# Residual update and norm by token tile, with the transposes queued behind set shares of context products

## The chip, the cores and the metric

The kernel is one program on one core of a Trainium2 chip. The metric is device time in microseconds. Before the change the median of three runs is 1722.03 us (1718.5 to 1724.54). The profile shown here was taken from one more execution, which took 1722.1 us.

## The reference, cut to what matters

256 tokens of 1024 features pass through two blocks, each with two layers. In the first block a layer is

```
u = rms_norm(h, g_mix_pre[i]);  y = mixer_i(u)          # i=0 stick-breaking, i=1 dilated
h = h + rms_norm(y, g_mix_post[i])
u = rms_norm(h, g_ffn_pre[i]);  f = relu(u @ w_ff_in)**2 @ w_ff_out
h = h + rms_norm(f, g_ffn_post[i])
h = h + (p[i] @ w_ple[i]) * sigmoid(rms_norm(h, g_ple[i]) @ w_ple_gate[i])
```

In the second block a layer works on the tokens and on 256 context tokens. Six rows of modulation per stream (shift, scale, gate, twice) come from a product of a condition vector:

```
u = rms_norm(h) * (1 + scale) + shift;  h = h + gate * mixer(u, context)   # i=0 MLA + pooling, i=1 grouped-query
u = rms_norm(h) * (1 + scale) + shift;  h = h + gate * conv_ffn(u)
```

The context goes through the same layer of its own at i=0 and gives keys and values at both. The result is the tokens after a last rms_norm with a gain. All is float32.

## The kernel before

**Products.** The 256 tokens are two tiles of 128, called tt = 0 and 1. Every float32 product is done as three products of rounded parts (`mm3`, L195 to L197: high by high, low by high, high by low). A weight block comes by a DMA that SyncE issues (`ws`, four buffers), is rounded on ScalarE (`wh`, L183), and VectorE subtracts to get the rest (`wl`, L184). Activations are split alike (`put_split`, L200 and L201). A normalised activation is transposed on TensorE into a PSUM bank of 512 columns (`flip_group`, L231), four transposes of 128 columns for a group, two groups for a token tile, and each group is then split into `uh` and `ul`. There are two banks `mm` and two banks `fx`.

**Stages.** On the main path the order is stick mixer, FFN, gate from p ("ple"), dilated mixer, FFN, ple, MLA, gated FFN ("ffn2"), grouped-query attention ("gqa"), gated FFN. Between two of them stands a stage end: the residual update from the two accumulators `acc` (`post_norm`, `gated_add`, or the end of `ple`), then `main_norm`, which makes the next `u` and transposes it. Both tiles are updated first, then both are normed, and each group's transposes are issued as soon as that half of `u` is made.

**Context work as filler.** The context's products and the modulation products (`fx` banks) don't hang on the main path. They are generators in the queues `ctx` and `mod`. `fill(n)` adds n microseconds' worth of credit and issues steps while the credit is above zero; each step takes its worth away. `FILL[...]` holds the amounts: after `main_norm` comes `fill(FILL["mix0"])` and so on for mix1 (8.5 each), post0 9.6, post1 12.0, ple0 and ple1 10.0, f2 15.0, pre2 8.5. A scheduler then orders each engine's instructions by readiness and priority, so transposes and filler products end up interleaved. `tc.issue_after(x)` adds an edge that holds what is issued under it behind instruction x. At the end of the last gqa stage and after it no context work is left.

**Second layer's context.** `ctx_norm` reads the context, `xc`, back from DRAM, where the end of the context's FFN at i=0 has written it (L1256, L1194), norms it tile by tile and transposes into the `fx` banks. `ffn2(0)` issues filler after each chunk until that norm is issued.

**Rows.** Gains, shifts and gates are loaded by `row`, broadcast over the partitions, 512 KB each, into one pool of two buffers; so the third row's DMA waits for the readers of the first. SyncE issues DMAs in the order written by the scheduler, and one that waits holds those behind it.

**The lines.** `post_norm` (L519) is a rstd, a mul and a scalar_tensor_tensor; `gated_add` is L527 and L528; the norm's Square is L223, its tensor_scalar L215, the power on GpSimd L217, the gain L245, and the last step L252 or L254.

Of the kernel before, what the change touches and what calls it, by code (L numbers as in the profile page):

```python
# [101 lines left out]
def two_block_kernel(ctx: ExitStack, tc: tile.TileContext, a: dict, out: bass.AP, dbg=None):  # L102
# [90 lines left out]

    def mm3(o, lh, ll, rh, rl, start, stop):
        pe.matmul(o, lh, rh, start=start, stop=False)  # L195
        pe.matmul(o, lh, rl, start=False, stop=False)  # L196
        pe.matmul(o, ll, rh, start=False, stop=stop)  # L197
# [44 lines left out]
    def norm_one(src, g, shift, f, tt, bank):  # L242
# [4 lines left out]
        c0 = 0  # L247
        for grp in f.groups:
            w = grp[0].shape[1] * 128
            s = slice(c0, c0 + w)  # L250
# [36 lines left out]
    def tok_blocks(y, us, blocks, first, last):  # L287

        for tt in range(2):
            ts = slice(tt * 128, (tt + 1) * 128)  # L290
            for k, ((uh, ul), (bh, bl)) in enumerate(zip(us, blocks)):
                for nh in range(2):
                    s = slice(nh * 512, nh * 512 + 512)
                    mm3(y[tt][:, s], uh[:, ts], ul[:, ts], bh[:, 0, s], bl[:, 0, s],
                        first and k == 0, last and k == len(us) - 1)
# [410 lines left out]
    def ple(i, u, pw):  # L706
        y = lin_tok(u, KC, a["w_ple_gate"][i])
        for tt in range(2):
            t = tmp()
            act.activation(out=t, in_=y[tt], func=AF.Sigmoid)  # L710
            vec.tensor_mul(out=t, in0=t, in1=pw[:, tt, :])
            vec.tensor_add(out=h[:, tt, :], in0=h[:, tt, :], in1=t)

# [694 lines left out]
    u = main_norm(g_first)  # L1408

    for i in range(2):  # L1410
        y = stick(u) if i == 0 else dilated(u)
        g = row(a["g_mix_post"][i])
        for tt in range(2):
            post_norm(y[tt], g, tt)
        save(f"h{i}a", h)
        u = main_norm(row(a["g_ffn_pre"][i]))
        fill(FILL[f"mix{i}"])
        with tc.tile_pool(name="pl", bufs=1) as p:
            pf = []
            y = ffn1(i, u, lambda: pf.append(ple_in(i, p)))  # L1420
            pw = ple_mm(i, p, pf[0])
            g = row(a["g_ffn_post"][i])
            for tt in range(2):
                post_norm(y[tt], g, tt)
            save(f"h{i}b", h)
            u = main_norm(row(a["g_ple"][i]))
            fill(FILL[f"post{i}"])
            until_dense(FILL[f"dp{i}"])
            ple(i, u, pw)
        save(f"h{i}c", h)  # L1430
        if i == 0:
            u = main_norm(row(a["g_mix_pre"][1]))
            fill(FILL["ple0"])
    u = main_norm(mod_row(0, 0, 1), mod_row(0, 0, 0))
    fill(FILL["ple1"])
# [14 lines left out]
    for i in range(2):  # L1450
        if i == 1:
            u = main_norm(mod_row(1, 0, 1), mod_row(1, 0, 0))
            fill(FILL["pre2"])
            y = gqa(u)
        g = mod_row(i, 0, 2)
        for tt in range(2):
            gated_add(y[tt], g, tt)
        save(f"xl{i}a", h)
        u = main_norm(mod_row(i, 0, 4), mod_row(i, 0, 3))
        fill(FILL["f2"])  # L1460
        y = ffn2(i, u)
        g = mod_row(i, 0, 5)
        for tt in range(2):
            gated_add(y[tt], g, tt)
        save(f"xl{i}b", h)
    g = row(a["g_final_2"])
    for tt in range(2):
        r = rstd(h[:, tt, :], D)
        t = tmp()
        vec.scalar_tensor_tensor(out=t, in0=h[:, tt, :], scalar=r, in1=g, op0=ALU.mult, op1=ALU.mult)  # L1470
        nc.sync.dma_start(out=out[0, tt * 128:(tt + 1) * 128, :], in_=t)
# [33 lines left out]
```

## Time and profile before

| | |
|---|---|
| median of three runs | 1722.03 us (1718.5 to 1724.54) |
| profiled execution: time, span | 1722.1 us, 1720.3 us |
| TensorE busy, matmuls | 1635.5 us, 95% |
| VectorE busy | 1211.1 us, 70% |
| ScalarE busy | 926.6 us, 54% |
| GpSimd busy | 44.6 us, 3% |
| DMA moved, mean | 337.65 MB, 196 GB/s |
| mean granted clock of TensorE | 0.988 of full |

A page gives the busy time of each engine, the span in 40 slices, and the chain of work that ended last. PE is TensorE's matmuls and PEld its weight loads, DVE VectorE, ACT ScalarE, POOL GpSimd, SP SyncE. In a timeline row the bracket is the idle time of that engine ahead of the row, with what ended it. Names are those of the program, without buffer numbers.

### The profile page before, as it was taken

The page shows a single profiled execution, that of the slowest core. Times are in us where ns is not written, and L with a number is a line of the kernel's source. Part 1 is how long each engine was busy: PE and PEld are TensorE (multiplying, and loading weights), DVE is VectorE, ACT ScalarE, POOL GpSimd, SP SyncE. Part 2 cuts the span into 40 slices and gives each one's busy share as a digit, 9 for nine tenths or more (in the row PEclk, how much of TensorE's full clock was granted, in tenths as well). Part 3 has the DMA queues.
Part 4 walks back from the last instruction along what each step waited for, and adds up shares of the span by engine and source line. Part 5 has one row for each costly group of instructions (what it writes and reads, how often), then busy time and mean ns, then how long its engine had stood idle before and what let it go on. Part 6 is the DMA issues. An engine that isn't in the chain of part 4 may idle for free.

```text
span 1720.3 us, 28310 instructions
## 1 busy us (share of the span) xinstructions
PE 1635.5 (95%) x10259; PEld 1428.7 (83%) x10260; DVE 1211.1 (70%) x2251; ACT 926.6 (54%) x1854; POOL 44.6 (3%) x69
## 2 busy tenths in 40 slices
PE   7998999999999999989989999999999999989997
PEld 6767888887788879877978898888989987779997
DVE  4437777678788886767767866867686687676665
ACT  5536555545655556544446555764555555545554
POOL 0000000000000000000000000000000000000000
PEclk9999999999999999999999999999999999989999
DMA  7777666665766665777876555345776664246662
GB/s 240 259 257 232 203 217 214 207 217 165 241 186 205 185 188 160 242 236 245 280 231 208 176 172 174 115 136 180 233 239 205 185 187 148 72 153 187 186 187 98
DMA packets 301039, 337.65 MB, mean 196 GB/s; under 512 B 18384, under 2 KB 246164, under 8 KB 300900
## 3 DMA queue, kind: packets, MB, share of 16 engines
q1 hardware_dynamic: 300900, 335.86, 62.4%
q8 instruction: 80, 1.31, 0.3%
q14 instruction: 59, 0.48, 0.1%
HBM read 332.56 MB, written 3.23 MB: 195 GB/s over the span
## 4 chain that ended last, share of the span: by engine, by line
PE 55%; DVE 14%; DMA 13%; issue 4%; ACT 3%; SPq 1%; POOL 1%; ACTq 0%; POOLq 0%; DVEq 0%
PE mm L195 6%; PE mm L196 6%; PE mm L197 6%; PE acc L197 6%; PE acc L196 6%; PE acc L195 6%; DMA ws<-in_w_mod 6%; DVE wl L184 5%; PE fx L195 4%; PE fx L196 4%; PE fx L197 4%; DMA ws<-in_w_ff_in 2%; DVE ga L497 2%; DMA ws<-in_w_in_dil 2%; ACT wh L183 1%
## 5 line engine op out<-in xcount | busy, mean ns | idle before, releaser
L184 DVE TENSOR_TENSOR wl<-ws,wh 128x512 fp32r<-128x512 f32 (+1 forms) x1004 | 638.1, 668 | 273.3 <-ACT wh L183 261.5
L183 ACT CAST wh<-ws 128x512 fp32r<-128x512 f32 (+1 forms) x1004 | 568.6, 604 | 477.8 <-PE mm L196 132.7
L197 PE MATMUL mm<-uh,wl 128*128 128x256 f32 x1344 | 382.9, 285 | 8.4 <-DVE wl L184 8.1
L195 PE MATMUL mm<-uh,wh 128*128 128x256 f32 x1344 | 382.3, 284 | 0.3
L196 PE MATMUL mm<-ul,wh 128*128 128x256 f32 x1344 | 381.5, 284 | 0.0
L197 PEld LDWEIGHTS mm<-uh,wl 128*128 128x128 f32 x1344 | 258.6, 192 | 11.5 <-DVE wl L184 11.0
L195 PEld LDWEIGHTS mm<-uh,wh 128*128 128x128 f32 x1344 | 258.7, 193 | 5.0 <-DVE ul L201 0.9
L196 PEld LDWEIGHTS mm<-ul,wh 128*128 128x128 f32 x1344 | 258.7, 193 | 2.6
L195 PE MATMUL acc<-wh,hh 128*128 128x512 f32 x432 | 172.1, 399 | 0.0
L196 PE MATMUL acc<-wl,hh 128*128 128x512 f32 x432 | 171.3, 397 | 0.0
L197 PE MATMUL acc<-wh,hl 128*128 128x512 f32 x432 | 170.2, 394 | 0.0
L497 DVE SCALAR_TENSOR_TENSOR ga<-ws,cst,ga 128x1024 f32<-128x1024 f32 x84 | 106.3, 1281 | 57.7 <-DMA ws<-in_w_mod 57.5
L195 PE MATMUL fx<-uch,wh 128*128 128x256 f32 x352 | 102.2, 290 | 0.0
L197 PE MATMUL fx<-uch,wl 128*128 128x256 f32 x352 | 100.9, 287 | 0.0
L196 PE MATMUL fx<-ucl,wh 128*128 128x256 f32 x352 | 100.5, 286 | 0.0
L197 PEld LDWEIGHTS acc<-wh,hl 128*128 128x128 f32 x432 | 81.9, 190 | 18.9 <-issue 1.2
L195 PEld LDWEIGHTS acc<-wh,hh 128*128 128x128 f32 x432 | 82.2, 190 | 17.6 <-issue 1.6
L196 PEld LDWEIGHTS acc<-wl,hh 128*128 128x128 f32 x432 | 82.3, 191 | 14.5
L195 PE MATMUL mm<-wh,uh 128*128 128x384 f32 (+1 forms) x256 | 85.3, 333 | 1.9 <-ACT wh L183 1.1
L196 PE MATMUL mm<-wl,uh 128*128 128x384 f32 (+1 forms) x256 | 83.0, 324 | 0.3 <-DVE wl L184 0.3
L197 PE MATMUL mm<-wh,ul 128*128 128x384 f32 (+1 forms) x256 | 82.0, 322 | 0.0
L217 POOL TENSOR_TENSOR s<-s,neghalf 128x1 f32<-128x1 f32 (+2 forms) x52 | 39.9, 767 | 1452.9 <-DVE s L215 1413.1
(405 smaller groups left out, 2705.8 us busy)
## 6 DMA issues: line engine op xcount, KB each, us to landing
ws<-in_ffn_w_up SPq DMA_DIRECT2D x528, 128.0 KB
ws<-in_w_mod SPq DMA_DIRECT2D x96, 512.0 KB
ws<-in_ffn_w_down SPq DMA_DIRECT2D x66, 512.0 KB
ws<-in_w_ff_in SPq DMA_DIRECT2D x64, 512.0 KB
ws<-in_w_ff_out SPq DMA_DIRECT2D x64, 512.0 KB
ws<-in_w_in_dil SPq DMA_DIRECT2D x96, 192.0 KB
ws<-in_w_in_sb SPq DMA_DIRECT2D x24, 512.0 KB
row<-mod SPq DMA_DIRECT2D x19, 512.0 KB
```

Source lines behind the costliest of these rows:

```text
L183: act.copy(out=h[:, s], in_=st[:, s])
L184: vec.tensor_sub(out=l[:, s], in0=st[:, s], in1=f32(h[:, s]))
L195: pe.matmul(o, lh, rh, start=start, stop=False)
L196: pe.matmul(o, lh, rl, start=False, stop=False)
L197: pe.matmul(o, ll, rh, start=False, stop=stop)
L217: gp.tensor_tensor(out=r, in0=v, in1=neghalf.to_broadcast([128, w]), op=ALU.pow)
L497: vec.scalar_tensor_tensor(out=o, in0=st, scalar=c, in1=o, op0=ALU.mult, op1=ALU.add)
```

## The change

1. `norm_vec` makes both halves of `u` for one tile without transposing. `main_norm` now takes the residual update as `pre` and does update and norm for tile 0, then for tile 1.
2. `fill_dense(n)` issues context steps worth n microseconds and gives back the last matmul. In `main_norm` tile 0's eight transposes are held behind the last matmul of a share FILL − 2.2, tile 1's eight behind that of a second share of 2.2; then comes `fill(2.2 + what was left)`. `fill_dense` sets the credit to what it has spent, so it is negative when it returns.
3. `gated_norm` loads the gate of the second block's residual updates into a pool of its own, opened after the stage before has closed its pools.
4. `tok_blocks` sorts a last block by output half. gqa's last output blocks are (4), (5, 6, 7) where they were (4), (5), (6, 7).
5. The first step: x's tile 0, the identity, the gain and then x's tile 1 are loaded in this order, and tile 1 is transposed into the `fx` banks.
6. The last step: gated update, sum of squares, scaling and output go by halves of 512 columns.

```diff
+    def norm_vec(src, g, shift):
         u = tmp()
         if shift is not None:
             vec.tensor_mul(out=u, in0=src, in1=g)
         r = rstd(src, D)
+        for s in (slice(0, 512), slice(512, 1024)):
...
-            flip_group(u[:, s], grp, tt, bank)
-            c0 += w
+        return u
@@ tok_blocks
-            for k, ((uh, ul), (bh, bl)) in enumerate(zip(us, blocks)):
-                for nh in range(2):
...
+            steps = [(k, nh) for k in range(len(us)) for nh in range(2)]
+            if last:
+                steps.sort(key=lambda x: x[1])
+            for k, nh in steps:
...
+    def fill_dense(n):
+
+        clean("mod")
+        last_mm[0] = None
+        while n > 0 and queues["ctx"] and dense[0] > 0.1:
+            before = credit["ctx"]
+            fill_step("ctx")
+            n -= before - credit["ctx"]
+        credit["ctx"] = min(credit["ctx"], 0.0)
+        return last_mm[0], n
@@ first loads
+    nc.sync.dma_start(out=ident, in_=ca[:, C_ID:C_ID + 128])
+    g_first = row(a["g_mix_pre"][0])
     nc.sync.dma_start(out=h[:, 1, :], in_=a["x"][0, 128:256, :])
-    g_first = row(a["g_mix_pre"][0])
-    nc.sync.dma_start(out=ident, in_=ca[:, C_ID:C_ID + 128])
@@ gqa
-            for ks in ((4,), (5,), (6, 7)):
+            for ks in ((4,), (5, 6, 7)):
@@
-    def main_norm(g, shift=None):
+    def main_norm(g, shift=None, pre=None, n=(0.0, 0.0, 0.0), banks=(mm1, mm1)):
+
         u = Feat(m4, KC, "u")
+        toks, left = [], 0.0
         for tt in range(2):
-            norm_one(h[:, tt, :], g, shift, u, tt, mm1)
+            if pre:
+                pre(tt)
+            toks.append(norm_vec(h[:, tt, :], g, shift))
+        for tt in range(2):
+            ins, more = fill_dense(n[tt] + left) if n[tt] else (None, 0.0)
+            left = max(more, 0.0)
+            with tc.issue_after(getattr(ins, "ins", ins)) if ins is not None else nullcontext():
+                to_T(toks[tt], u, tt, banks[tt])
+        fill(left + n[2])
         return u
...
+    def filler(name):
+        return (FILL[name] - 2.2, 2.2, 2.2)
+
+    def gated_norm(y, i, m, j, k, name):
+
+        with tc.tile_pool(name="rw", bufs=1) as p:
+            gate = p.tile([128, D], F32, name="gate")
+            nc.sync.dma_start(out=gate, in_=mod[i][0, m * D:(m + 1) * D].partition_broadcast(128))
+            return main_norm(mod_row(j, 0, k + 1), mod_row(j, 0, k), pre=behind(y, gate, gated_add), n=filler(name))
 
     for i in range(2):
         y = stick(u) if i == 0 else dilated(u)
-        g = row(a["g_mix_post"][i])
-        for tt in range(2):
-            post_norm(y[tt], g, tt)
+        u = main_norm(row(a["g_ffn_pre"][i]), pre=behind(y, row(a["g_mix_post"][i]), post_norm), n=filler(f"mix{i}"))
         save(f"h{i}a", h)
-        u = main_norm(row(a["g_ffn_pre"][i]))
-        fill(FILL[f"mix{i}"])
...
@@ last step
+        for nh in range(2):
+            s = slice(nh * 512, nh * 512 + 512)
+            vec.tensor_mul(out=t[:, s], in0=y[tt][:, s], in1=gate[:, s])
+            vec.tensor_add(out=h[:, tt, s], in0=h[:, tt, s], in1=t[:, s])
+            act.activation(out=j[:, s], in_=h[:, tt, s], func=AF.Square, accum_out=ss[:, nh:nh + 1])
...
+        for nh in range(2):
+            s = slice(nh * 512, nh * 512 + 512)
+            vec.scalar_tensor_tensor(out=t[:, s], in0=h[:, tt, s], scalar=r, in1=g[:, s], op0=ALU.mult, op1=ALU.mult)
+            nc.sync.dma_start(out=out[0, tt * 128:(tt + 1) * 128, s], in_=t[:, s])
```

Three places show what the edit does to the order of the instructions.

TensorE before, at the end of the first mixer: `fx` are context products, the rows with `ident` are transposes of `t`, the normed tile 0.

```order
L197 MATMUL fx<-wh,ucl 128x512
L231 MATMUL mm<-ident,t_1948 128x128 x4
L195 MATMUL fx<-wh,uch 128x512
L231 MATMUL mm<-ident,t_1948 128x128 x4
L196 MATMUL fx<-wl,uch 128x512
L197 MATMUL fx<-wh,ucl 128x512
L195 MATMUL fx<-wh,uch 128x512
L196 MATMUL fx<-wl,uch 128x512
L197 MATMUL fx<-wh,ucl 128x512
L195 MATMUL fx<-wh,uch 128x512
L231 MATMUL mm<-ident,t_1972 128x128 x4
```

Each group of four transposes has products of the filler behind it. Tile 1's two groups follow in the same way, and six products of filler stand between the second of tile 0 and the first of tile 1.

TensorE after, at the same place, the end of the second share; `t_1958` is the normed tile 1, and `mm<-uh` are the FFN's own products.

```order
L197 MATMUL fx<-wh,uch 128x512
L198 MATMUL fx<-wl,uch 128x512
L199 MATMUL fx<-wh,ucl 128x512
L233 MATMUL mm<-ident,t_1958 128x128 x8
L197 MATMUL mm<-uh,wh 128x256
L198 MATMUL mm<-ul,wh 128x256
L199 MATMUL mm<-uh,wl 128x256
```

All eight transposes of a tile stand together, 36 filler products are ahead of tile 0's and 12 between the tiles, and behind tile 1's the FFN's own products follow with no filler between.

SyncE before, from the last weights of the first gated FFN on: `gr` is a gain of the gqa stage, `row` a shift or a scale.

```order
L177 DMA ws<-in_ffn_w_down 128x1024 x3
L177 DMA ws<-in_gqa_w_in 128x2x512 x6
L1260 DMA gr<-in_gqa_g_q 128x128
L206 DMA row<-mod_118 128x1024
L177 DMA ws<-in_gqa_w_in 128x2x512
L206 DMA row<-mod_118 128x1024 x2
L177 DMA ws<-in_gqa_w_in 128x2x512
```

The gate is a row that was loaded earlier here, ahead of this stretch.

SyncE after, at the same place, from the write of the context to DRAM on.

```order
L1274 DMA xc_120<-xc 128x1024
L208 DMA row<-mod_118 128x1024
L1274 DMA xc_120<-xc 128x1024
L1212 DMA xc<-xc_120 128x1024
L177 DMA ws<-in_ffn_w_down 128x1024
L177 DMA ws<-in_gqa_w_in 128x2x512 x3
L1212 DMA xc<-xc_120 128x1024
L177 DMA ws<-in_gqa_w_in 128x2x512 x2
L208 DMA row<-mod_118 128x1024
L1448 DMA gate<-mod_117 128x1024
L208 DMA row<-mod_118 128x1024
L177 DMA ws<-in_gqa_w_in 128x2x512 x3
```

The gate's load stands behind the second read of `xc` and ahead of the third batch of gqa weights. Its pool lies where the FFN's pool was, and it waits for the last product that reads that pool, the last of the FFN.

VectorE after, at the end of that FFN: `L542` is the gate's mul and `L543` the add to `h`, `t_14905` the context's tile 1, `ucl` its split, `t_15092` the normed tile 0 of the tokens.

```order
L253 SCALAR_TENSOR_TENSOR t_14905<-t_14905,s,row 128x512 x2
L184 TENSOR_TENSOR wl<-ws,wh 128x512 x2
L203 TENSOR_TENSOR ucl<-fx,uch 128x4x128 x2
L184 TENSOR_TENSOR wl<-ws,wh 128x512
L542 TENSOR_TENSOR t_15089<-acc,gate 128x1024
L184 TENSOR_TENSOR wl<-ws,wh 128x512
L543 TENSOR_TENSOR h<-h,t_15089 128x1024
L184 TENSOR_TENSOR wl<-ws,wh 128x512
L247 TENSOR_TENSOR t_15092<-h,row 128x1024
L217 TENSOR_SCALAR s<-s 128x1
L542 TENSOR_TENSOR t_15103<-acc,gate 128x1024
L253 SCALAR_TENSOR_TENSOR t_15092<-t_15092,s,row 128x512 x2
```

The mul with the gate stands behind the split of the context's second tile; the norm of tile 0 is done between the two tiles' muls.

## Rows read from the trace of the kernel before

**Rows 1.** The page: busy times, DMA total, chain by engine

```profile
PE 1635.5 (95%) x10259; PEld 1428.7 (83%) x10260; DVE 1211.1 (70%) x2251; ACT 926.6 (54%) x1854; POOL 44.6 (3%) x69
...
DMA packets 301039, 337.65 MB, mean 196 GB/s; under 512 B 18384, under 2 KB 246164, under 8 KB 300900
...
PE 55%; DVE 14%; DMA 13%; issue 4%; ACT 3%; SPq 1%; POOL 1%; ACTq 0%; POOLq 0%; DVEq 0%
```

**Rows 2.** Groups by line, TensorE, transposes: busy, mean ns, idle before, releasers

```profile
L231 PE MATMUL mm<-ident,t 128*128 128x128 f32 x170 | 30.7, 314 | 27.4 <-DVE t L252 11.5 <-DVE t L254 10.7 <-DVE ul L201 3.9
L231 PE MATMUL fx<-ident,t 128*128 128x128 f32 x58 | 9.6, 285 | 5.4 <-DVE t L254 2.6 <-DVE s L215 2.1 <-ACT wh L183 0.4
```

**Rows 3.** Windows at stage ends: length, each engine's busy time, clock, DMA, GB/s

```profile
191.00:200.00 9.00, 8.56 (x42) 6.87 (x42) 8.12 (x14) 7.83 (x15) 2.40 (x3) 1.00 0.33 119
439.00:448.00 9.00, 8.84 (x46) 6.77 (x45) 8.56 (x16) 6.94 (x14) 1.72 (x2) 1.00 0.57 192
474.00:486.00 12.00, 11.93 (x60) 9.42 (x59) 10.62 (x17) 9.10 (x17) 1.79 (x2) 1.00 0.23 66
685.00:698.00 13.00, 11.09 (x56) 8.46 (x56) 12.29 (x20) 9.23 (x17) 2.02 (x3) 1.00 0.36 108
903.00:916.00 13.00, 12.15 (x75) 10.52 (x74) 12.01 (x20) 11.07 (x22) 2.96 (x4) 1.00 0.58 184
945.00:958.00 13.00, 9.91 (x77) 9.25 (x77) 11.76 (x17) 8.57 (x16) 1.48 (x2) 0.98 0.38 116
956.00:960.00 4.00, 2.04 (x10) 2.05 (x11) 3.43 (x8) 0.90 (x2) 0.55 (x1) 0.69 0.42 137
960.00:964.00 4.00, 4.00 (x30) 3.84 (x30) 3.69 (x8) 2.90 (x6) 0.00 (x0) 0.89 0.69 215
1168.00:1186.00 18.00, 15.89 (x73) 11.95 (x72) 16.60 (x23) 10.21 (x18) 2.55 (x2) 1.00 0.50 162
1408.00:1412.00 4.00, 2.22 (x9) 1.45 (x9) 4.00 (x14) 1.55 (x10) 1.41 (x2) 0.93 0.76 242
1516.00:1522.00 6.00, 4.17 (x16) 3.00 (x16) 5.55 (x10) 1.76 (x3) 0.94 (x1) 0.50 0.66 216
```

**Rows 4.** Timeline, end of the gqa stage: start, busy, engine, idle before

```profile
1509.76 0.39 PE L197 MATMUL acc<-wh,o 128*128 128x512 f32 x1
1516.56 1.94 PE L231 MATMUL mm<-ident,t 128*128 128x128 f32 x8 [6.41 <-DVE t L254]
1517.69 0.59 ACT L200 CAST uh<-mm 128x512 fp32r<-128x512 f32 x1 [2.49 <-PE mm L231]
1518.86 0.68 DVE L201 TENSOR_TENSOR ul<-mm,uh 128x512 fp32r<-128x512 f32 x1
1519.60 2.38 PE L231 MATMUL mm<-ident,t 128*128 128x128 f32 x8 [1.10 <-DVE ul L201]
1522.12 0.58 PE L195 MATMUL mm<-uh,wh 128*128 128x256 f32 x1
```

**Rows 5.** Chain that ended last, context norm inside the first second-block FFN

```profile
1258.48 0.23 PE fx L197
1266.10 5.69 DMA xc<-xc
1274.92 0.66 PE fx L231 x4
```

**Rows 6.** Timeline, end of the program

```profile
1709.91 0.39 PE L197 MATMUL acc<-wh,hl 128*128 128x512 f32 x1
1714.75 0.55 POOL L217 TENSOR_TENSOR s<-s,neghalf 128x1 f32<-128x1 f32 x1 [1.53 <-DVE s L215]
1715.34 1.28 DVE L1470 SCALAR_TENSOR_TENSOR t<-h,s,row 128x1024 f32<-128x1024 f32 x1 [0.73 <-POOL s L217]
```

**Rows 7.** Timeline, start of the program, TensorE

```profile
8.86 1.97 PE L231 MATMUL mm<-ident,t 128*128 128x128 f32 x8 [8.86 <-DVE t L252]
12.77 2.31 PE L231 MATMUL mm<-ident,t 128*128 128x128 f32 x8 [1.94 <-DVE ul L201]
```

More of the change, by code (lines that the diff above doesn't have):

```diff
@@ L1 @@
-from contextlib import ExitStack
+from contextlib import ExitStack, nullcontext
 import numpy as np
@@ L290, in tok_blocks @@
             ts = slice(tt * 128, (tt + 1) * 128)
[L291 to L295 removed]
+            steps = [(k, nh) for k in range(len(us)) for nh in range(2)]
+            if last:
+                steps.sort(key=lambda x: x[1])
+            for k, nh in steps:
+                (uh, ul), (bh, bl) = us[k], blocks[k]
+                s = slice(nh * 512, nh * 512 + 512)
+                mm3(y[tt][:, s], uh[:, ts], ul[:, ts], bh[:, 0, s], bl[:, 0, s],
+                    first and k == 0, last and k == len(us) - 1)
     def lin_tok(u, n, w, order=None, y=None):
@@ L707, in ple, with add @@
         y = lin_tok(u, KC, a["w_ple_gate"][i])
-        for tt in range(2):
+        def add(tt):
             t = tmp()
@@ L712, in ple @@
             vec.tensor_add(out=h[:, tt, :], in0=h[:, tt, :], in1=t)
+        return add
     def ple_in(i, p):
@@ L1407, in two_block_kernel, with behind @@
     queues["ctx"].extend([g_ctx, g_ctx1])
-    u = main_norm(g_first)
+    u = main_norm(g_first, banks=(mm1, fx1))
+    def behind(y, g, f):
+        return lambda tt: f(y[tt], g, tt)
+    def filler(name):
[5 more added lines that the diff above has]
+            return main_norm(mod_row(j, 0, k + 1), mod_row(j, 0, k), pre=behind(y, gate, gated_add), n=filler(name))
     for i in range(2):
         y = stick(u) if i == 0 else dilated(u)
-        g = row(a["g_mix_post"][i])
-        for tt in range(2):
-            post_norm(y[tt], g, tt)
+        u = main_norm(row(a["g_ffn_pre"][i]), pre=behind(y, row(a["g_mix_post"][i]), post_norm), n=filler(f"mix{i}"))
         save(f"h{i}a", h)
-        u = main_norm(row(a["g_ffn_pre"][i]))
-        fill(FILL[f"mix{i}"])
         with tc.tile_pool(name="pl", bufs=1) as p:
@@ L1421, in two_block_kernel @@
             pw = ple_mm(i, p, pf[0])
-            g = row(a["g_ffn_post"][i])
-            for tt in range(2):
-                post_norm(y[tt], g, tt)
+            u = main_norm(row(a["g_ple"][i]), pre=behind(y, row(a["g_ffn_post"][i]), post_norm), n=filler(f"post{i}"))
             save(f"h{i}b", h)
-            u = main_norm(row(a["g_ple"][i]))
-            fill(FILL[f"post{i}"])
             until_dense(FILL[f"dp{i}"])
-            ple(i, u, pw)
-        save(f"h{i}c", h)
[L1431 to L1435, printed above, removed]
+            add = ple(i, u, pw)
+            if i == 0:
+                u = main_norm(row(a["g_mix_pre"][1]), pre=add, n=filler("ple0"))
+            else:
+                u = main_norm(mod_row(0, 0, 1), mod_row(0, 0, 0), pre=add, n=filler("ple1"))
+        save(f"h{i}c", h)
     while "kT" not in ctxk:
@@ L1450, in two_block_kernel @@
     for i in range(2):
-        if i == 1:
-            u = main_norm(mod_row(1, 0, 1), mod_row(1, 0, 0))
-            fill(FILL["pre2"])
-            y = gqa(u)
[L1455 to L1466, printed above, removed]
+        u = gated_norm(y, i, 2, i, 3, "f2")
+        save(f"xl{i}a", h)
+        y = ffn2(i, u)
+        if i == 0:
+            u = gated_norm(y, 0, 5, 1, 0, "pre2")
+            save("xl0b", h)
+            y = gqa(u)
+    gate, g = mod_row(1, 0, 5), row(a["g_final_2"])
     for tt in range(2):
-        r = rstd(h[:, tt, :], D)
         t = tmp()
-        vec.scalar_tensor_tensor(out=t, in0=h[:, tt, :], scalar=r, in1=g, op0=ALU.mult, op1=ALU.mult)
-        nc.sync.dma_start(out=out[0, tt * 128:(tt + 1) * 128, :], in_=t)
+        j = tmpp.tile([128, 1024], BF16, tag="junk", name="junk", bufs=1)
+        ss = small(2)
+        for nh in range(2):
[3 more added lines that the diff above has]
+            act.activation(out=j[:, s], in_=h[:, tt, s], func=AF.Square, accum_out=ss[:, nh:nh + 1])
+        sq = small()
+        vec.tensor_add(out=sq, in0=ss[:, 0:1], in1=ss[:, 1:2])
+        r = rstd_of(sq, D, 1)
+        for nh in range(2):
+            s = slice(nh * 512, nh * 512 + 512)
+            vec.scalar_tensor_tensor(out=t[:, s], in0=h[:, tt, s], scalar=r, in1=g[:, s], op0=ALU.mult, op1=ALU.mult)
+            nc.sync.dma_start(out=out[0, tt * 128:(tt + 1) * 128, s], in_=t[:, s])
+    save("xl1b", h)
 _INS = ["x", "p", "positions", "w_in_sb", "w_out_sb", "w_in_dil", "w_out_dil", "g_mix_pre", "g_mix_post",
```

10 lines of the change are left out of this document (4 added, 6 removed).

## The prediction

> **What bounds the kernel now.** I read the page first, then the groups by line for the transposes, then windows around each stage end, then timelines where a window showed a hole. The reader is to see in the page that TensorE's matmuls are busy for 1635.5 of 1720.3 us and that the chain that ended last is TensorE for 55% [rows 1]. So all the idle time of TensorE is 85 us, and the change, which neither adds nor removes a product, can only move that. In the groups, the 170 issues of main-path transposes have 27.4 us of idle time ahead of them, the 58 of the context's 5.4 us [rows 2]. Of the 27.4 us, 8.86 is the wait for the first input and 1.94 the bank at the start [rows 7], 6.41 and 1.10 lie at the end of gqa, where no filler is left [rows 4]. What is left, 27.4 − 8.86 − 1.94 − 6.41 − 1.10 = 9.1 us, is spread over the ends that have filler. The windows say where: length minus PE busy is 0.44, 0.16, 0.07, 1.91, 0.85, 3.09 and 2.11 us at mix0, post0, ple0, mix1, post1, ple1 and f2 of i=0, in all 8.6 us, and 1.78 us at pre2 [rows 3]. VectorE is busy for 12.29 of 13 us at mix1 and 16.60 of 18 at f2 [rows 3], so there the norm chain is limited by VectorE's own work, not by what it waits for.
>
> **The seven ends with filler.** The change puts tile 0's chain (update and norm) wholly ahead of tile 1's, and holds the transposes behind 36 context products of 0.23 us [rows 5], 8.3 us, or as much in narrower ones. At the end of gqa both updates and tile 0's norm together take 6.4 us after the last product [rows 4], so within 8.3 us tile 0 is normed, and the waits on `t` in [rows 2] go: 8.6 us. In return the filler that stood behind the last transposes is gone at four ends, since `fill_dense` returns with a negative credit and the third fill seldom issues: at mix0, mix1, ple1 and f2 the next stage's products, which need both tiles, follow at once. They wait for the split of the first bank, ScalarE 0.59 and then VectorE 0.68 us, less four transposes that still run. The nearest row is the end of gqa, where TensorE waits 1.10 us for such a split [rows 4]. Four such waits cost 4.4 us; bounds are 0 (a filler product slips in) and 4 × (0.59 + 0.68) = 5.1 us. After post0, post1 and ple0 tile 0's products or a mask come first and I take nothing.
>
> Two smaller gains belong here. After the hole at ple1 the granted clock is 0.69 for 4 us and 0.89 for 4 us more [rows 3], so (0.31 + 0.11) × 4 = 1.7 us went there at most, and 1.3 if the idle part of the first window is left out. The Trainium skill (TensorE: Matmul & The Clock Gate, "The HAM clock gate") says that the throttled clock is the default and that activity releases it, so that a hole costs more than its length; the trace agrees here (0.69), and at the end of gqa, where 6.41 us of idle time are followed by 0.50 of full, which is 1.2 GHz [rows 3, 4]. But the hole of f2 leaves the clock at 1.00 [rows 3], so this is no price for every hole. The second gain is the interleaving: four transposes between products take 0.66 us [rows 5], while in a row of eight one takes 1.94 / 8 = 0.24 us at half clock [rows 4], by my estimate 0.12 at full and 0.48 for four, so a group costs some 0.15 us for switching in and out; each end has two groups fewer, 7 × 2 × 0.15 = 2 us. Sum of this part: −8.6 + 4.4 − 1.3 − 2 = −7.5 us; bounds −13 (no wait for splits) and −2 (VectorE, 95% busy at mix1, is late with tile 1 by half of what it is late now).
>
> **The end of the first gated FFN (pre2).** Here the change costs. First, the negative credits delay the context's FFN, so its last product stands near the end of this stage and no longer in its first half. From that product to the first transposes of the context norm it took 1274.92 − 1258.71 = 16.2 us before, 5.69 of them the read of `xc` [rows 5]. In the new order some 17 wide and 96 narrow products stand between, 17 × 0.23 + 96 × 0.12 = 15.4 us: a stall of 0.8. The second tile's read is queued on SyncE behind three weight loads, and VectorE has some 8 us of splits and weights to do ahead of that tile's norm, against 31 products (7.1 us) and eight transposes: 1 to 3 us more, I take 2. Then the filler waits for the split of that tile, 1.10 by [rows 4], or 1.9 with two `wl` ahead of it in VectorE's queue; 1.5. Second, the gate. Its load waits on SyncE for the stage's last product and has a row and two weight blocks in flight ahead of it. At 196 GB/s [rows 1] one 512 KB block takes 2.7 us, so it lands some 5 us after the last product (bounds 2.7 and 3 × 2.7 = 8). From there mul, add, Square, power and the halves take about 8 us, and TensorE has the second tile's transposes, its split and 36 products, some 13 us after the end, so tile 0 is on time. Tile 1's chain has 12 products and 3 of gqa behind tile 0's, 3.4 us, against VectorE's add, gain, split and last step of 4.7 us: 1.3. The last split is 1.1. Together 0.8 + 2 + 1.5 + 1.3 + 1.1 = 6.7, against 1.8 now: +4.9 us. Bounds 0 (tile 1's read early, all splits hidden) and +11 (gate at 8 us, and half clock after it).
>
> **The other edits.** The end of gqa has no filler to queue behind. There the product order lets tile 0's accumulator end 18 products before the last, not 12, worth 6 × 0.23 = 1.4 us, but the gate waits on SyncE for the last score product and stands behind weight loads, and VectorE is busy without a break through the whole 6.41 us; I take 0, bounds −1.4 and +2. At the program's end 1716.62 − 1710.30 = 6.3 us follow the last product [rows 6]; halves start the Square earlier, but VectorE's order puts tile 0's last two steps, which wait for GpSimd, between tile 1's halves; +0.5, bounds −0.8 and +1.5. At the start the second tile's transposes no longer wait for a bank (1.94 us, [rows 7]), but tile 0's last step is queued behind tile 1's sum of squares, whose input is now loaded last; 0, bounds −1.9 and +1.5. The stages between are full with or without filler (4.00 of 4.00 at 960 us, [rows 3]), so moved filler costs nothing there; where it is bunched, at the end of the first FFN, up to +2.
>
> **Sum.** −7.5 + 4.9 + 0.5 = −2.1 us on the profiled execution's 1722.1: 1720.0. That run is 0.1 us above the median of 1722.03, so the same forecast stands against the median. Within 0.3%, or 5.2 us, this kernel's measurement can't tell a change; the forecast is in that band.
>
> **Rivals.**
> A, faster: the splits stay covered and pre2 is no worse than now. The page's VectorE share of 70% [rows 1] speaks for it, its 95% in the window at mix1 [rows 3] against it. Then −13 + 0.5 = −12.5 at the full size, and −8 where half of it comes: 1710 to 1714.
> B, slower: the gate's load becomes the bound at the ends of the FFN and of gqa. It decides once the gate lands more than 5 us after the last product at pre2, since tile 0 then comes after its 36 products. With 8 us there are 3 us more, with half clock behind them as at the end of gqa (0.50, [rows 3]) 2 to 3 us more, and 2 at the end of gqa: 1720 + 8 = 1728. For it speaks that weights share the 196 GB/s, against it that the DMA share is only 0.76 at 1408 us and 0.50 at f2 [rows 3]. The Trainium skill (DMA: Bandwidth & Descriptors, "Anatomy of one DMA") says that a DMA's wait is done on the issuing sequencer; no row here shows it for this load, and by it the three blocks behind the gate would start late too.
> C, the change doesn't do what it says: with the credit negative the shares only borrow from later fills, and VectorE's work, unchanged in amount, sets each end. Then the ends give −2, pre2 takes +5 and the rest +1.5: 1726, still in the band.
>
> **How the numbers follow.** My forecast 0.38, C 0.12, A 0.30, B 0.20. Of the first two together 0.42 lies within the band, 0.05 below and 0.03 above it. So faster by over 0.3% (under 1716.9) is 0.35, within it 0.42, slower (over 1727.2) 0.23. The forecast's own range is 1717 to 1726. The range for 8 in 10 reaches to A's upper half and B's price: 1710 to 1729.
>
> **What would show it.** In the changed profile the seven windows should have 4 to 5 us of idle time in all, the transposes of the main path waits on `ul` and not on `t`, the clock 1.00 at ple1. Around pre2 the transposes into `fx` wait for `t` twice and the first product behind them for `ucl`; 6 to 7 us in all. The mul with the gate waits for a DMA. I am wrong if pre2's holes are under 2 us or over 10, or if main transposes still wait for `t` at mix1, ple1 and f2.

## The result and the profile after

The changed kernel takes 1741.96 us (median, 1740.57 to 1746.47) against 1720.26 us (1716.18 to 1724.54): ratio 1.0135, 95% interval [1.0103, 1.0168]. The forecast was 1720.0 with a range of 1710 to 1729, so the time lies outside it, on the side of rival B. The profiled execution has a span of 1744.6 us, 24.3 more than before.

The page after, in the lines that answer to [rows 1]:

```profile
PE 1644.7 (94%) x10260; PEld 1439.2 (82%) x10260; DVE 1210.2 (69%) x2259; ACT 923.3 (53%) x1857; POOL 40.6 (2%) x69
...
PE 52%; DVE 16%; DMA 13%; issue 5%; ACT 3%; SPq 1%; POOL 1%; DVEq 0%; POOLq 0%; ACTq 0%
```

The chain is less TensorE (52% against 55%) and more VectorE. The transposes after, as groups by line (busy, mean ns, idle before, releasers), against [rows 2]:

```profile
L233 PE MATMUL mm<-ident,t 128*128 128x128 f32 x162 | 25.4, 299 | 22.1 <-DVE t L251 10.5 <-DVE t L253 7.9 <-DVE ul L203 1.7
L233 PE MATMUL fx<-ident,t 128*128 128x128 f32 x66 | 11.5, 305 | 5.7 <-DVE t L253 3.6 <-DVE s L217 1.6 <-ACT wh L183 0.4
```

The idle time ahead of main-path transposes fell from 27.4 to 22.1 us. Of the 22.1 us, 10.29 is the wait for the first input and 4.06 + 3.42 lie at the end of gqa, so 4.3 are left where it was 9.1 before. So the waits that the change aimed at did shrink, the way that was forecast, and the 24 us stand elsewhere. Windows at the stage ends after (mix0, ple0, mix1, ple1, f2, pre2; length, busy times, clock, DMA), against [rows 3]:

```profile
195.00:207.00 12.00, 10.09 (x52) 7.91 (x51) 11.49 (x20) 9.17 (x18) 2.02 (x3) 1.00 0.78 249
490.00:497.00 7.00, 5.30 (x33) 4.07 (x32) 6.56 (x14) 3.78 (x8) 0.66 (x1) 1.00 0.78 238
697.00:712.00 15.00, 8.90 (x42) 7.03 (x41) 12.43 (x23) 6.89 (x14) 0.55 (x1) 0.89 0.68 229
964.00:981.00 17.00, 12.70 (x74) 11.02 (x74) 14.64 (x28) 9.51 (x19) 0.93 (x1) 0.90 0.61 185
1180.00:1200.00 20.00, 15.31 (x79) 13.48 (x80) 14.60 (x28) 8.60 (x17) 0.00 (x0) 0.83 0.70 215
1398.00:1436.00 38.00, 32.26 (x153) 24.48 (x152) 32.77 (x60) 21.97 (x49) 3.90 (x6) 0.96 0.65 213
```

Length minus PE busy is 1.91, 1.70, 6.10, 4.30, 4.69 and 5.74 us. At mix1, ple1 and f2 the granted clock is below full as well, 0.89, 0.90 and 0.83, where before only ple1 had lost some.

To add this up over the program I compared the two traces product by product. The main path has 7543 products in the same order in all kernels. For each matmul, the distance from its start to the next start, less the usual distance of its shape in the kernel before (the 30th percentile), is idle or slow time (slow where the clock is below full); summed between the same two main-path products it gives each stage's share, whatever filler lies there. The table has us more than before, at the ends alone:

| end | after | x1 | x2 | x3 | x4 | x7 | x12 |
|---|---|---|---|---|---|---|---|
| mix0 | 0.98 | 0.98 | 0.98 | −0.11 | 1.44 | 0.01 | 0.84 |
| post0 | −0.20 | −0.65 | −0.18 | −0.63 | 0.42 | 0.03 | 0.65 |
| ple0 | 1.36 | 1.36 | 1.34 | 0.01 | 1.52 | 0.00 | 1.52 |
| mix1 | 5.27 | 1.23 | 2.61 | 0.19 | 2.38 | 0.00 | 1.81 |
| post1 | −0.14 | −1.43 | −0.63 | 0.14 | 0.25 | 0.00 | 0.29 |
| ple1 | 1.85 | 3.61 | −1.62 | 1.11 | 0.43 | 0.15 | 0.38 |
| f2 | 6.37 | 3.55 | 1.92 | 0.72 | 1.37 | 1.48 | −0.53 |
| pre2 | 3.04 | 1.64 | 3.19 | 0.99 | 3.02 | 6.05 | −1.54 |
| gqa's end | 0.85 | 0.90 | 1.25 | 2.50 | 2.05 | 1.67 | 0.67 |
| sum | 19.4 | 11.2 | 8.9 | 4.9 | 12.9 | 9.4 | 4.1 |

(x1 to x12 are the experiments below.) Inside the stages the same sums move by several us either way from one kernel to the next, also where the order is the same, so a single profile says little there; the verdicts below rest on the timed runs, and the table says only where.

The place with the largest new hole that no row of before had is mix1. Its timeline after, in order of time (all engines; `acc` the stage's last product):

```profile
690.04 0.39 PE L199 MATMUL acc<-wh,o 128*128 128x512 f32 x1
694.48 1.41 DVE L251 SCALAR_TENSOR_TENSOR t<-h,s,row 128x512 f32<-128x512 f32 x2 [0.44 <-POOL s L219]
700.36 0.42 ACT L1142 ACTIVATE cv<-cv 128x256 f32<-128x256 f32 x1 [0.24 <-DVE s L217]
700.79 0.55 POOL L219 TENSOR_TENSOR s<-s,neghalf 128x1 f32<-128x1 f32 x1 [4.21 <-DVE s L217]
701.38 1.41 DVE L251 SCALAR_TENSOR_TENSOR t<-h,s,row 128x512 f32<-128x512 f32 x2 [0.45 <-POOL s L219]
702.71 0.42 DVE L1143 TENSOR_TENSOR cv<-fx,cv 128x256 f32<-128x256 f32 x1
703.18 0.79 PE L197 MATMUL fx<-wh,hch 128*128 128x512 f32 x1 [4.93 <-DVE cv L1143]
705.91 1.36 PE L233 MATMUL mm<-ident,t 128*128 128x128 f32 x8
711.37 0.39 PE L197 MATMUL mm<-uh,wh 128*128 128x256 f32 x1 [1.16 <-DVE ul L203]
```

Tile 0's last step on VectorE ends at 694.48 + 1.41 = 695.89, 5.5 us after the stage's last product. Its transposes start at 705.91, 10.0 us later, since they are held behind the first share. The share is late: its product at 703.18 has waited 4.93 us for `cv`, the last step of the context FFN's convolution. That step stands on VectorE at 702.71, behind the last step of tile 1's norm (701.38). Its input from ScalarE was done at 700.36 + 0.42 = 700.78, but VectorE stood idle for 0.45 us until GpSimd had finished tile 1's power, and then did the norm first. So in VectorE's order tile 1's update and norm are ahead of the filler's own work, and in TensorE's order the filler is ahead of the transposes of tile 0, which was ready. Behind the hole the granted clock is 0.57 from 703 to 707 us. At 711.37 the split of the last bank costs 1.16 us more, the wait of 1.1 that was forecast.

f2 after shows the same twice, `wl` and `cv`, then the transposes, then the split; the first row is the last step of tile 0's norm:

```profile
1174.18 1.41 DVE L253 SCALAR_TENSOR_TENSOR t<-t,s,row 128x512 f32<-128x512 f32 x2 [0.44 <-POOL s L219]
1181.71 0.58 PE L199 MATMUL fx<-uch,wl 128*128 128x256 f32 x1 [3.36 <-DVE wl L184]
1192.65 0.50 PE L197 MATMUL fx<-wh,hch 128*128 128x512 f32 x1 [1.83 <-DVE cv L1143]
1194.14 1.04 PE L233 MATMUL mm<-ident,t 128*128 128x128 f32 x8
1197.10 1.09 PE L233 MATMUL mm<-ident,t 128*128 128x128 f32 x8
1199.33 0.39 PE L197 MATMUL mm<-uh,wh 128*128 128x256 f32 x1 [1.14 <-DVE ul L203]
```

Here tile 0 is normed at 1175.59 and its transposes start at 1194.14, 18.6 us later; at ple1 they start 9.8 us after tile 0's norm, behind a wait of the filler of 2.85 us for `wl`.

### The profile page after: what moved, and what is told of

Its sections match the earlier page's. It is cut to its first block, busy times and chain, and to the rows that moved or that the text cites. A ratio compares the mean times of both kernels' runs of the same rounds, so it can differ in the third digit from the quotient of the medians.

```text
span 1744.6 us, 28338 instructions
## 1 busy us (share of the span) xinstructions
PE 1644.7 (94%) x10260; PEld 1439.2 (82%) x10260; DVE 1210.2 (69%) x2259; ACT 923.3 (53%) x1857; POOL 40.6 (2%) x69
## 4 chain that ended last, share of the span: by engine, by line
PE 52%; DVE 16%; DMA 13%; issue 5%; ACT 3%; SPq 1%; POOL 1%; DVEq 0%; POOLq 0%; ACTq 0%
DMA ws<-in_w_mod 7%; PE mm L197 7%; PE mm L198 7%; PE mm L199 7%; PE acc L199 6%; PE acc L198 6%; PE acc L197 6%; DVE wl L184 6%; PE fx L197 3%; PE fx L199 3%; PE fx L198 3%; DVE ga L512 3%; DMA ws<-in_w_ff_in 2%; ACT wh L183 1%; SPq L177 1%
## 5 line engine op out<-in xcount | busy, mean ns | idle before, releaser
L199 PEld LDWEIGHTS fx<-uch,wl 128*128 128x128 f32 x352 | 70.3, 200 | 6.6 <-DVE wl L184 6.6
```

Source lines behind the costliest of these rows:

```text
L199: last_mm[0] = pe.matmul(o, ll, rh, start=False, stop=stop)
```

## The experiments

Ratios are against the kernel before, run on the same chip.

**x1_no_debt.**

```diff
+        owed = credit["ctx"]
...
-        credit["ctx"] = min(credit["ctx"], 0.0)
+        credit["ctx"] = min(owed, 0.0) + min(n, 0.0)
...
-        return (FILL[name] - 2.2, 2.2, 2.2)
+        return (FILL[name] - 2.2, 2.2, 0.0)
```

> The changed kernel, but the shares issued by fill_dense are paid from the share itself, so the credit isn't left negative by more than the overshoot, and the third fill is dropped (the sum per stage end is FILL, as before). Theory D (the negative credit starves the stages, so that the context stands at other places when a stage end comes, and the filler there is a chain of up-product, convolution and down-product in place of ready products): the waits of filler on cv and wl at mix1, ple1 and f2 (4.9, 3.7 and 1.8 us) go, 1729 to 1733 us. Theory H (the hold: transposes wait behind filler although the normed tile is ready): only what the context's place changes, 1738 to 1742. Theory T (the order by tile keeps VectorE from the filler's own work): 1740.

Measured 1735.51 us, 1.0081 [1.0051, 1.0110]. It gains 0.5%, less than theory D said and more than the others did. At f2 the filler still waits, now for sums and weights of the context, and the next stage's first product waits longer for the split (TensorE rows of this kernel):

```profile
1183.40 0.50 PE L197 MATMUL fx<-wh,hch 128*128 128x512 f32 x1 [1.34 <-DVE fsum L1266]
1187.65 0.50 PE L198 MATMUL fx<-wl,hch 128*128 128x512 f32 x1 [0.81 <-DVE wl L184]
1205.58 0.39 PE L197 MATMUL mm<-uh,wh 128*128 128x256 f32 x1 [2.54 <-DVE ul L203]
```

**x2_no_hold.**

```diff
-            with tc.issue_after(getattr(ins, "ins", ins)) if ins is not None else nullcontext():
-                to_T(toks[tt], u, tt, banks[tt])
+            to_T(toks[tt], u, tt, banks[tt])
```

> The changed kernel with the same shares and credit, but without the edge that holds the transposes behind the last product of a share. Theory H: the transposes go as soon as a tile is normed, filler that waits no longer holds them, 1728 to 1734 us. Theory D: the filler still waits for itself, 1737 to 1742. Theory T: 1738 to 1742.

Measured 1735.29 us, 1.0077 [1.0051, 1.0103]: just above the 1728 to 1734 us of theory H. Its profiled run was the fastest of its seven (span 1727.8 us), so its column in the table is rather low. f2 shows the mechanism; TensorE rows of this kernel:

```profile
1178.47 1.03 PE L233 MATMUL mm<-ident,t 128*128 128x128 f32 x8
1180.52 0.50 PE L197 MATMUL fx<-wh,hch 128*128 128x512 f32 x1 [1.01 <-DVE cv L1143]
```

The filler waits for `cv` as in the changed kernel, but the transposes now go ahead of it, and the wait is 1.01 us in place of 1.83 with transposes held behind it. The wait for `wl` is still there too, 2.48 us at 1170.71 in place of 3.36.

**x3_old_norm.**

```diff
-            toks.append(norm_vec(h[:, tt, :], g, shift))
...
+        if pre:
+            for tt in range(2):
+                pre(tt)
+        for tt in range(2):
...
+        fill(sum(n) - n[2])
```

> The changed kernel with main_norm as before: both updates, then both norms with the transposes behind each half, then one fill of FILL. The gate's own pool, the first and last step and the product order stay as changed. All theories: what is left is the end of the first gated FFN and small edits, 1722 to 1728 us; if it stays above 1735 the cause lies in the gate's pool or the product order and not in main_norm.

Under the last loop stand the gain, the rstd, each half and its transposes, as in the kernel before. Measured 1727.6 us, 1.0039 [1.0015, 1.0064], inside the expectation. `main_norm` is the larger part of the loss, about two thirds; some 7 us remain without it.

**x4_tile_only.**

```diff
         for tt in range(2):
             if pre:
                 pre(tt)
             toks.append(norm_vec(h[:, tt, :], g, shift))
-        for tt in range(2):
-            ins, more = fill_dense(n[tt] + left) if n[tt] else (None, 0.0)
...
+            to_T(toks[tt], u, tt, banks[tt])
+        fill(sum(n) - n[2])
```

> The changed kernel with update and norm by tile, but the transposes issued at once and one fill of FILL behind them: neither shares, hold nor negative credit. Theories H and D: as x3_old_norm or better, 1718 to 1727 us. Theory T: 1735 to 1742.

Measured 1735.87 us, 1.0077 [1.0053, 1.0102]: neither hold nor shares nor negative credit ("debt"), and still some 13 us slower. My theories H and D both fell here as the whole cause; theory T, which I had put up as a rival, holds for a part. The gate's pool and the small edits are still in this kernel, as in x3, so the order by tile adds 0.77 − 0.39 = 0.4%. x1, x2 and x4 agree within 0.04%, so each cure of the shares leads back to the time of x4. They agree in the total only: at mix1 the table has 1.23, 2.61 and 2.38 us, at f2 3.55, 1.92 and 1.37.

**x5_start.** The four first loads reordered and tile 1's bank changed in the kernel before:

```diff
+    nc.sync.dma_start(out=ident, in_=ca[:, C_ID:C_ID + 128])
+    g_first = row(a["g_mix_pre"][0])
     nc.sync.dma_start(out=h[:, 1, :], in_=a["x"][0, 128:256, :])
...
-    u = main_norm(g_first)
+    u = main_norm(g_first, banks=(mm1, fx1))
```

> The kernel before with the first step alone changed: x's tile 0, the identity, the gain, x's tile 1, and tile 1's transposes into the fx banks. In every kernel so far that has this edit the first product of the first projection starts with 2.7 us less idle time than before; in the stretch up to the first mixer's end 1.9 of it come back in one of them and 2.5 more are won in another. Theory S (the edit is a gain of its own): 1717.5 to 1719, 0.1 to 0.2% less than before. Rival: the projection behind it is bound by its weights, and the whole is given back, 1720 to 1721.

Measured 1721.5 us, 1.0001 [0.9980, 1.0022]. No gain shows, and not for the rival's reason alone. The second wait for a bank is gone, but VectorE now has tile 1's rstd step (at 11.05 us), whose input is loaded last, ahead of tile 0's last step, so the first transposes start at 11.98 us in this trace, 8.86 before [rows 7]. The first product starts at 15.48, 15.30 before; the 200th at 45.7, 43.9 before. In the changed kernel's trace they start at 13.8 and 44.0, so there an earlier first product was given back within 200 products.

**x6_updates_first.**

```diff
-        for tt in range(2):
-            if pre:
-                pre(tt)
+        if pre:
+            for tt in range(2):
+                pre(tt)
+        for tt in range(2):
             toks.append(norm_vec(h[:, tt, :], g, shift))
```

> The changed kernel with both residual updates ahead of both norms, as before; shares, hold and negative credit as changed. Theory T (the order by tile costs 8 us, since tile 1's chain no longer runs in the latency of tile 0's): 1733 to 1736 us. Theory H and D alone (shares, hold and credit cost what was measured, the order nothing): 1739 to 1742.

Measured 1754.3 us, 1.0188 [1.0163, 1.0214]. Both expectations missed, and on the far side: under the hold the order by tile saves 0.5% (1.0188 against 1.0135, with intervals that overlap by 0.0005). At mix0 the traces show where. The first product of the next stage, here and in the changed kernel:

```profile
207.25 0.39 PE L197 MATMUL mm<-uh,wh 128*128 128x256 f32 x1 [2.35 <-DVE ul L203]
```

```profile
206.85 0.39 PE L197 MATMUL mm<-uh,wh 128*128 128x256 f32 x1 [1.15 <-DVE ul L203]
```

With both updates first, tile 1 is normed sooner, at 201.78 against 204.40 us, and the held transposes are no later. But VectorE then takes four weight blocks (204.11 to 206.59) ahead of the last split. The idle time is not much larger, 2.35 us in one piece against 0.21 + 0.55 + 1.15 = 1.9 in three; the clock granted from 207 to 212 us is 0.66 against 1.00, which is some 1.7 us. At ple0 it is 0.82 against 1.00 from 490 to 497 us. So the order costs where nothing is held, and saves where it is.

**x7_gate_pool.** In the kernel before, no other edit:

```diff
-        g = mod_row(i, 0, 2)
-        for tt in range(2):
-            gated_add(y[tt], g, tt)
+        with tc.tile_pool(name="rw", bufs=1) as p:
+            gate = p.tile([128, D], F32, name="gate")
...
+            for tt in range(2):
+                gated_add(y[tt], gate, tt)
```

> The kernel before with the gates of the second block loaded into a pool of their own; nothing else. Theory G (the gate's load waits for the last products and holds the queue, at the ends of the first gated FFN and of gqa): x3_old_norm lost 7 us with this and the small edits, so 1724 to 1727 us. Rival (the 7 us are the product order in gqa and the last step): 1719 to 1722.

Measured 1732.07 us, 1.0055 [1.0036, 1.0075], more than expected. At pre2 of this kernel, SyncE's issue of the gate, VectorE's two muls, TensorE's transposes:

```profile
1396.62 0.34 SPq L1453 DMA_DIRECT2D gate<-mod  x1
```

```profile
1400.98 2.36 DVE L527 TENSOR_TENSOR t<-acc,gate 128x1024 f32<-128x1024 f32 x2 [2.41 <-DMA gate<-mod]
```

```profile
1409.19 1.32 PE L231 MATMUL mm<-ident,t 128*128 128x128 f32 x8 [1.72 <-DVE t L254]
1412.05 2.38 PE L231 MATMUL mm<-ident,t 128*128 128x128 f32 x8 [1.02 <-DVE ul L201]
```

The gate is issued at 1396.62 and used at 1400.98, 4.4 us later, near the 5 us of the prediction; VectorE waits 2.41 us for it while the updates could have run, both tiles are late, and the filler is used up before the transposes (1.72, then 1.02 for the split, then at a granted clock of 0.50 from 1412 to 1418 us).

**x8_no_debt_no_hold.** The edits of x1 and x2 together.

> The changed kernel with the credit kept whole and without the edge that holds the transposes: shares are only issued ahead of the transposes in the program. Each alone gave 6.5 us. If debt and hold are two causes, the gains add: 1728 to 1730 us. If they are one (held transposes stand behind filler that is late, and either cure is enough): 1734 to 1737, where the order by tile alone stood.

Measured 1737.0 us, 1.0079 [1.0056, 1.0102]. The gains do not add. Hold and negative credit act only together: both at once cost 1.0135 − 1.0079, some 10 us (the intervals just miss each other); either alone adds nothing to x4 in the total. That does not mean that no wait is left. At f2 of this kernel the next stage's first product waits for the split, which stands behind weight blocks in VectorE's queue:

```profile
1202.91 0.58 PE L197 MATMUL mm<-uh,wh 128*128 128x256 f32 x1 [4.22 <-DVE ul L203]
```

**x9_gate_early.**

```diff
...
+            with tc.tile_pool(name="gatep", bufs=1) as own:
+                y = ffn2(i, u)
+                u = gated_norm(y, 0, 5, 1, 0, "pre2", own)
...
```

> The changed kernel with the pool of the one gate at the end of the first gated FFN opened ahead of that FFN, so that the load doesn't wait for the FFN's last product. Theory G (the pool's place makes the load late; alone in the kernel before it added 6.05 us of idle time there): the 4 us that the changed kernel has more in that FFN and at its end shrink to 1, 1736 to 1739 us against 1742 for the changed kernel. Rival (at this place the context's round trip and the hold set the end): the idle time there stays, 1741 to 1743.

Measured 1745.73 us, 1.0129 [1.0091, 1.0168]: no gain shows. The timed runs alone can't tell the 3 us in question, but the trace can: by the sums of the table some 3.2 of the 4.0 us that the changed kernel has more in that FFN and at its end stay. The rival holds. TensorE rows of this kernel at pre2, the gate already there:

```profile
1399.56 1.32 PE L233 MATMUL fx<-ident,t 128*128 128x128 f32 x8 [1.43 <-DVE t L253]
1409.38 1.29 PE L233 MATMUL fx<-ident,t 128*128 128x128 f32 x8 [0.93 <-DVE t L253]
1411.68 0.50 PE L197 MATMUL fx<-wh,uch 128*128 128x512 f32 x1 [1.02 <-DVE ucl L203]
```

The context's two tiles and the split of the second wait much as they did in the changed kernel (below). Here the mul with the gate runs at 1407.36 without a wait, tile 0's transposes are held until 1423.37, and the filler ahead of them waits twice for `wl`, 1.57 and 0.81 us. So in the changed kernel the late gate is hidden behind the context and the hold.

**x10_hold_plain.**

```diff
     def filler(name):
+        if name in ("mix1", "post1", "ple1", "f2"):
+            return (0.0, 0.0, FILL[name])
         return (FILL[name] - 2.2, 2.2, 2.2)
```

> The changed kernel with shares and hold only at mix0, post0, ple0 and pre2, where the filler is projections of the context; at mix1, post1, ple1 and f2, where the filler may be the context's gated FFN with its convolution, the transposes are not held and one fill of FILL follows. Theory H in its narrow form (a held transpose is late where the filler ahead of it waits for VectorE): mix1, ple1 and f2 fall from 5.3, 1.9 and 6.4 us more than before to 2.4, 0.4 and 1.4, as with the order by tile alone, 1731 to 1735 us. Rival (the hold costs as much with plain filler, by pushing it out of the stages): 1738 to 1742.

Measured 1742.94 us, 1.0107 [1.0075, 1.0139]. Inconclusive: the time is far above theory H's range and just above the rival's. In its trace the three ends fall to 3.29, 0.95 and 2.64 us more than before, most of the way to what was expected, but the ratio moves by 0.3% only, with intervals that overlap those of the changed kernel and of x8. The idle time inside the first mixer was 5.9 us more than before in this one profile.

**x11_small_edits.**

```diff
-        with tc.tile_pool(name="rw", bufs=1) as p:
-            gate = p.tile([128, D], F32, name="gate")
...
+        gate = mod_row(i, 0, m)
+        for tt in range(2):
+            gated_add(y[tt], gate, tt)
```

(on top of x3_old_norm)

> The changed kernel with main_norm as before and the gates loaded as rows of the shared pool, as before: what is left of the change are the first step, the product order in the last blocks and the last step by halves. If the gate's pool was all that x3_old_norm lost, this is the kernel before within 0.15%, 1718 to 1723 us. If the small edits cost part of it, 1724 to 1727.

Measured 1722.54 us, 1.0013 [0.9990, 1.0037]. First step, product order and last step are worth nothing that can be told from zero; the program's tail after its last main-path product went from 10.65 to 11.96 us in the traces, the only sign of the +0.5 forecast.

**x12_tile_block1.** In the kernel before, at the six ends of the first block:

```diff
-    def main_norm(g, shift=None):
+    def main_norm(g, shift=None, pre=None):
         u = Feat(m4, KC, "u")
         for tt in range(2):
+            if pre:
+                pre(tt)
             norm_one(h[:, tt, :], g, shift, u, tt, mm1)
...
```

> The kernel before with update and norm by tile at the six ends of the first block only; the transposes are not held, fill and credit stay as before, the second block too. Theory T: x4_tile_only stood 8 us above x3_old_norm, and by idle time 5 to 6 of it at these six ends, so 1725 to 1728 us. Rival (those 8 us came from the gate's pool together with the order, in the second block): 1719 to 1723.

Measured 1728.31 us, 1.0042 [1.0021, 1.0063]; just above theory T's range; idle time at the six ends 5.5 us more, as expected. The cause stands on VectorE. At mix1, before: the first rstd step of the end, and the last half of tile 1's norm.

```profile
684.12 0.15 DVE L215 TENSOR_SCALAR s<-s 128x1 f32<-128x1 f32 x1 [1.91 <-ACT junk L223]
695.37 0.74 DVE L252 SCALAR_TENSOR_TENSOR t<-h,s,row 128x512 f32<-128x512 f32 x1
```

The same in x12_tile_block1, with the start of tile 0's second rstd step and of tile 1's update between:

```profile
691.31 0.15 DVE L215 TENSOR_SCALAR s<-s 128x1 f32<-128x1 f32 x1 [1.92 <-ACT junk L223]
696.11 0.15 DVE L215 TENSOR_SCALAR s<-s 128x1 f32<-128x1 f32 x1
700.52 1.27 DVE L523 SCALAR_TENSOR_TENSOR h<-t,s,h 128x1024 f32<-128x1024 f32 x1
703.95 1.41 DVE L252 SCALAR_TENSOR_TENSOR t<-h,s,row 128x512 f32<-128x512 f32 x2
```

From the first rstd step to the end of tile 1's last step it took 695.37 + 0.74 − 684.12 = 12.0 us before, and 703.95 + 1.41 − 691.31 = 14.05 us by tile. With both updates first, tile 1's update runs while ScalarE squares and GpSimd raises tile 0; by tile, tile 1's update (at 700.52 its second half) starts only when tile 0's last step is done. On TensorE the hole stands ahead of a filler product, while VectorE was busy with tile 1's update, tile 0's splits and the context's sums:

```profile
703.14 0.47 PE L195 MATMUL fx<-wh,hch 128*128 128x512 f32 x1 [3.08 <-ACT junk L223]
```

Tile 1's transposes follow without a wait. This end has 1.81 us of idle time more than before; that these are the 2.05 us of the longer chain is argued from their size.

## Why the prediction was wrong

**The step that failed is the seven ends with filler, −7.5 us.** By the table they measured 0.98 − 0.20 + 1.36 + 5.27 − 0.14 + 1.85 + 6.37 = +15.5 us, a miss of 23, about the whole difference of 22 between the forecast and the time. (1.5 of it, at f2, may be the gate's pool, by x7.) The prediction took the filler as a cover that is always ready: "36 context products of 0.23 us". That tile 0 is normed within them was right: at mix1 it took 5.5 us. Its parts came out like this.

- That the waits for `t` go: they did, in the rows of the transposes (27.4 to 22.1 us). But a held transpose does not show its wait. It is charged to the filler ahead of it, `cv` 4.93 at mix1 and 1.83 at f2, `wl` 2.85 at ple1 and 3.36 at f2. So neither of the signs named for being wrong appeared: no main transposes wait for `t` at mix1, ple1 and f2, and pre2's 5.74 us lie between 2 and 10. The idle time told it: in place of 4 to 5 us at the seven ends, five of them have 18.7 in the windows above.
- Four split waits of 1.1 us: 1.16 at mix1, 1.14 at f2 and 1.15 at mix0; right. At ple1 it is 0.32 and 0.22 for the two parts. I gave ple0 none, and it has 0.82 and 0.88.
- That tile 0's chain ahead of tile 1's only helps. I counted when tile 0 would be ready and not when tile 1 would; x12 shows 2.05 us later at mix1, and x4 against x3 puts it at 0.4% over the program. The prediction's own rows had VectorE 95% busy at mix1, and it used this for the lower bound of this term only.
- The 2 us for unbroken groups of transposes did not show: waits left out, the 112 transposes of the seven ends take 13.6 us before and 13.4 after, each from its start to the next start on TensorE.

The negative credit I did name, as what empties the third fill. That it moves the context to other places, so that at mix1 and f2 the shares are the chain of up-product, convolution and down-product and no longer ready products, I did not follow through; x1 and x8 show it matters only together with the hold. In steps from the kernel before, the timed runs give 0.39% for the edits other than `main_norm` (x3), 0.77% with the order by tile (x4), 0.79% with the shares as well (x8) and 1.35% with hold and negative credit.

**Pre2, +4.9 us, was near** in size: 3.04 at the end and 0.93 in the FFN ahead of it. TensorE rows after:

```profile
1404.06 1.32 PE L233 MATMUL fx<-ident,t 128*128 128x128 f32 x8 [2.12 <-DVE t L253]
1413.86 1.29 PE L233 MATMUL fx<-ident,t 128*128 128x128 f32 x8 [0.97 <-DVE t L253]
1416.24 0.55 PE L197 MATMUL fx<-wh,uch 128*128 128x512 f32 x1 [1.08 <-DVE ucl L203]
1426.14 1.17 PE L233 MATMUL mm<-ident,t 128*128 128x128 f32 x8
1431.13 1.29 PE L233 MATMUL mm<-ident,t 128*128 128x128 f32 x8 [0.38 <-DVE t L253]
```

The context's transposes wait 2.12 and 0.97 us (forecast 0.8 and 2), the filler behind them 1.08 (1.5), tile 0 has no wait, as forecast, tile 1 0.38 (1.3). That the gate would not set this end was right too: x9. VectorE did wait for it here, and longer at the end of gqa:

```profile
1419.38 1.23 DVE L542 TENSOR_TENSOR t<-acc,gate 128x1024 f32<-128x1024 f32 x1 [2.01 <-DMA gate<-mod]
1529.48 1.22 DVE L542 TENSOR_TENSOR t<-acc,gate 128x1024 f32<-128x1024 f32 x1 [4.31 <-DMA gate<-mod]
```

The mul at pre2 starts 6.5 us after the last product (1412.51 + 0.39), where the forecast had the gate 5 us after it.

**Rival B** named the gate's load as the mechanism of a slower kernel, at 1728. In the changed kernel it does not act at pre2 (x9), though the gate came later than the 5 us at which this rival was to decide; at the end of gqa VectorE waited 4.31 us for it, and that end lost 0.85. Put alone into the kernel before, it costs 0.55%, most of it at pre2. Without main_norm's change (x3) 0.39% remain, and 0.13%, not told from zero, when the gate's pool goes too (x11); so the pool is the likely cause of most of what x3 lost, if at other places: in the table pre2 has 6.05 us in x7 and 0.99 in x3, the end of gqa 1.67 and 2.50. **Rival A** fell. **Rival C** held in one half, that VectorE's work sets the ends, and missed that moving that work makes it longer.

**The clock.** At ple1 it is 0.90 over 17 us after, (1 − 0.90) × 17 = 1.7 us as before, so the 1.3 us of the prediction did not come. It cost time at two ends more. At mix1 it is 0.57 from 703 to 707 us, behind the hole of 4.93 us. At f2 it is 0.51 from 1182 to 1188 us, behind the hole of 3.36, and 1.00 from 1192 to 1200, behind the one of 1.83; before, 2.11 us of idle time in all had left it at 1.00 [rows 3]. By these shares 0.43 × 4 = 1.7 and 0.49 × 6 = 2.9 us of the +15.5 are the clock.

**The edits taken at nothing or near it** (start, gqa order, last step) were worth nothing that shows: x5 and x11.

What stays open: the order by tile costs 0.4% in x4 and x12 and saves 0.5% under the hold (x6 against the changed kernel), and only mix0 and ple0 were followed in the traces for it; how hold and credit share their 10 us was argued from two ends, not measured at each; and why x1, x2, x4 and x8 come to the same total with holes at different places is not shown.

## What to carry to other kernels

Filler that hides a chain on another engine must not need that engine: before a transpose is put behind filler products, look in the in-order queue of VectorE at what the filler itself needs and where it stands against the chain to be hidden. A sign of being wrong must be looked for where the wait will be charged: here on the filler, not on the held transposes. When a two-tile chain is reordered so that the first tile is ready earlier, work out when the second is ready, for the next stage needs both. A buffer placed where the last stage's pool lay was loaded only when the last reader was done (product at 1412.51, gate issued at 1412.97); with a pool opened earlier (x9) it was there in time.

## What the runs showed that was not expected

The order by tile changes sign with the hold: 0.4% slower without it (x12, [1.0021, 1.0063]), and with it 1.0135 against 1.0188. Also, idle time inside the stages moved by several us between kernels with the same order there (the first mixer, −2.7 in x9 and +5.9 in x10 against before), so single profiles of this kernel don't settle a per cent.
